# Reordering gate products, GpSimd weight steps and the last branch-B unit in a hybrid encoder block

## The chip, the cores and the metric

The kernel runs on one core of one Trainium2 chip. The metric is device time in microseconds (us) of one execution. The engines are called PE (TensorE, matrix products), PEld (PE's weight loads), DVE (VectorE), ACT (ScalarE), POOL (GpSimd) and SP (SyncE, which mostly issues DMA transfers).

## The reference, cut to what matters

One encoder block on 1024 tokens plus 16 meta tokens, model width 1024. One projection feeds two attention branches and two gates; the gated sum goes through an output projection and then a SwiGLU feed-forward.

```python
proj = h @ w_in                       # qa, ka, va, qb, kb, vb, ga, gb
y_a = differential_attention(qa, ka, va, ...)   # 4 heads, two score maps each, all 1040 keys
y_b = windowed_gqa(qb, kb, vb, sink)            # 8 heads in 2 groups, keys within 128
merged = jax.nn.sigmoid(ga) * (y_a @ w_ba) + jax.nn.sigmoid(gb) * (y_b @ w_bb)
h = h + merged @ w_o                  # then the feed-forward
```

The differential attention takes softmax(map 1) - lam * softmax(map 2), times v, and a norm over the head. All data are float32; the kernel splits each operand of a product into a high and a low part and adds three matmuls (high x high, high x low, low x high).

## The kernel before, in words

**Branch B** (`attend_b`, lines 363 to 465) works in units (g, t): group g, 128-token block t. A unit computes scores, softmax and transposes, and its `finish()` accumulates the values into one PSUM bank `bpy`. For the key tile with the meta tokens (k = 8) ACT makes the high part `bmh` (L443) and DVE the low part in four pieces, `btm` (L446); PE's first values matmul (L447) waits for these. At its end ACT copies one half of `bpy` (L459), DVE adds the other (L460), and SP stores the result to `yb_d` in DRAM (L461). Units overlap: the copy and add of unit (1,6) are queued in the middle of unit (1,7), the last.

**Branch A** (the loop of lines 1136 to 1178) works in 32 tiles: head h of 4, token block t of 8. A string of `SLOTS` gives the order of PE's steps in a tile: `s` is a scores step (matmuls L1028; DVE then takes L1031, L1035), `t` a group of transposes of the previous tile (`apt` L1057, taken by ACT L1060 and DVE L1061 into `at`), `n` a step of values or norm, and `g` a quarter of a gate product. Tiles 0 to 15 use the first two strings in turn, tiles 16 to 31 the third, `SLOTS[2]`.

**The gates** (lines 757 to 965) and half of the columns of qa are computed as 2 x 2 block products in the manner of Strassen and Winograd: each of nine column pairs k (0 to 7, and `Q_PAIR` = 8) takes seven products p. `order_g` lists them in two passes. The first, `first_g`, has products 1, 6 and 2 of each k; the second has products 5, 3, 7 and 4. A product is 4 steps of 3 matmuls (L921) against the transposed input `hT` (high and low parts in SBUF).
- Its weights are made on POOL by `weights_g`: block sums of the raw weights (L806 to L819), a rounded high part (L828) and a low part (L829). The four operand buffers are freed by PE; the raw weights are loaded by SP (`load_g`, L786).
- Its result is built up in one of two PSUM banks, `pp0` and `pp1`. Products 1 and 2 of a k share a bank, and so do 5 and 3, and 7 and 4. Between the two of a pair another engine reads the bank: ACT copies after 1 (L927) and 5 (`q`, L949), DVE adds after 6 (L945) and 7 (`g`, L952). Product 5 begins in a bank that ACT has loaded with a kept sum (L904).
- Between the passes SP replaces quarters of `hT` by block sums that were stored in DRAM as `t_d[0..3]` (`turn_into`, L853), each as soon as the last product that needs the old quarter is done (`LAST_T`).
- All other stores and loads of this stretch go through SP's one queue in program order.

The order in which the scheduler hands an instruction to an engine's queue is held by two means: `queue_behind` (one instruction after another on the same engine) and `tc.issue_after` blocks.

Of the kernel before, what the change touches and what calls it, by code (L numbers as in the profile page):

```python
# [74 lines left out]
def encoder_block(ctx: ExitStack, tc: tile.TileContext, x, meta, norm_mix, w_in, lq1, lk1, lq2, lk2,  # L75
# [289 lines left out]
    scaled = []  # L365
    last_unit, quarters = [], []

# [29 lines left out]
    def attend_b(g, t, qb):  # L397
# [33 lines left out]
        def finish():  # L431
            py = bank(psum1, "by", f"bpy_{nm}", 1)
            for k in [8, *range(b0, b1)]:
# [4 lines left out]
                if k == 8:  # L438
                    steps[-1].append(nc.tensor.transpose(pt[:, 0, :], md, ident))
                    steps.append([])  # L440
                    tm = tms[t % 2]
                    hi = bpool.tile([P, P], F32R, tag="bmh", name=f"bmh_{nm}", bufs=1)
                    nc.scalar.activation(hi, pt[:, 0, :], AF.Copy, scale=of_hi)  # L443
                    for r in range(4):
                        at = slice(32 * r, 32 * r + 32)
                        nc.vector.scalar_tensor_tensor(tm[at, r], pt[at, 0, :], of_x[at], f32(hi[at]), ALU.mult, ALU.subtract)  # L446
                    steps[-1].append(nc.tensor.matmul(py, vb[g][:, 8, :], tm.rearrange("p r t -> p (r t)"), start=True, stop=False))  # L447
                    continue
# [6 lines left out]
                for hl in range(2):  # L455
                    steps[-1].append(nc.tensor.matmul(py, vb[g][:, k, :], tr[:, hl].rearrange("p r t -> p (r t)"),  # L456
                                                      start=False, stop=(k == b1 - 1 and hl == 1)))
            y1 = bpool.tile([64, 512], F32, tag="by1", name=f"by1_{nm}", bufs=2)
            nc.scalar.copy(y1, py[64:128])  # L459
            nc.vector.tensor_tensor(y1, py[0:64], y1, ALU.add)  # L460
            nc.sync.dma_start(yb_d[g][:, t * P:(t + 1) * P].rearrange("(r d) t -> d r t", r=4),  # L461
                              y1.rearrange("d (r t) -> d r t", r=4))
        return finish
# [295 lines left out]
    for k in (2, 3, 4, 5, 6, Q_PAIR):  # L759
        first_g += [(k, 1), (k, 6), (k, 2)] + ([(0, 6)] if k == 6 else [])  # L760
    first_g += [(7, 1), (7, 2), (7, 6), (1, 6)]
    second_g = [Q_PAIR, *range(8)]
    behind_g = dict(zip(second_g, second_g[1:]))
    order_g = first_g + [(k, p) for k in second_g for p in (5, 3, 7, 4)]
    n_first = len(first_g)

    uses_g = []
    for n, (k, p) in enumerate(order_g):
        if n >= n_first:
            uses_g.append([("s", k, 1), ("s", k, 0)] if p == 5 else [])  # L770
        else:
            uses_g.append({1: [("f", k, 0)], 2: [], 6: [("f", k, 1)] if k >= N_SPLIT else [("m", k, 0), ("m", k, 1)]}[p])
    loads_g = [u for us in uses_g for u in us]
    raw_g, ops_g, n_loaded, n_freed, n_made = {}, {}, [0], [0], [0]

    def load_g():
        while n_loaded[0] < min(len(loads_g), n_freed[0] + 4):
            kind, k, i = key = loads_g[n_loaded[0]]
            p, tag = ((wpool, "w"), (gwork, "w2"))[n_loaded[0] // 2 % 2]
            n_loaded[0] += 1  # L780
            col = G_COLS[k] + i * P
            w = raw_g[key] = p.tile([P, DC, P], F32, tag=tag, name=f"wg_{kind}{k}_{i}", bufs=2)
            with ExitStack() as after:
                if n_loaded[0] > 4:
                    after.enter_context(tc.issue_after(keys_a[0].ins))
                raws_g.append(nc.sync.dma_start(w, w_in[:, col:col + P].rearrange("(c p) n -> p c n", p=P)))  # L786

    sums_g, keys_a, raws_g, values_in, turned_t, made_g = {}, [], [], [], {}, []

    def weights_g(n):  # L790
# [11 lines left out]
        elif p == 2:  # L802
            src = a12
            n_freed[0] += 1 if k < N_SPLIT else 2 if k != 7 else 0
        elif p == 6:
            tt(a21, a21, a22, ALU.add)  # L806
            tt(a21, a21, a11, ALU.subtract)
            src = a21
            if k < N_SPLIT or k == 7:
                n_freed[0] += 2  # L810
# [13 lines left out]
        op = ops_g[n] = wpool.tile([P, 2, 4, P], F32R, tag=("wh", "wl")[n % 2], name=f"wopg_{nm}", bufs=W_BUFS)  # L824
        with ExitStack() as after:
            if made_g:
                after.enter_context(tc.issue_after(made_g[-1].ins))
            nc.gpsimd.tensor_copy(op[:, 0], src)  # L828
            made_g.append(tt(op[:, 1], src, f32(op[:, 0]), ALU.subtract))  # L829
# [26 lines left out]
    def gate_steps():  # L856
# [1072 lines left out]
```

## Time and profile before

| | |
|---|---|
| median of 3 runs (range) | 1433.23 us (1431.43 to 1435.07) |
| profiled execution, its span | 1433.91 us, 1432.0 us |
| PE busy | 1405.1 us, 98% of the span |
| DVE, ACT, POOL busy | 927.9, 671.5, 656.4 us |
| longest stretch with PE never idle | 626.5 to 1425 |

An execution runs through the projections and branch B (to about 284 us), branch A with the gate products between its steps (284 to 626), the gated output projection and the feed-forward (from 626). A row of the profile's timeline gives start, duration, engine, line, operation and tiles; in brackets stands how long the engine sat idle before it and what ended the wait.

### The profile page before, as it was taken

Reading aid. Unit: us, or ns where it says so; the run is one execution under the profiler, and the core shown is the slowest. Engines: PE = TensorE matmul, PEld = TensorE weight load, DVE = VectorE, ACT = ScalarE, POOL = GpSimd, SP = SyncE. Lnnn points to the kernel's source line nnn. Section 1 sums busy time; section 2 is a strip of 40 time slices with the busy share of each in tenths; the row PEclk is TensorE's granted clock in tenths of the full one; section 3 lists DMA queues with packets and bytes.
Section 4 is the critical chain, followed back from the end, with each engine's and each line's share of the span. In section 5 each row is a group of like instructions: output and inputs, shape, how many; then the busy total and the mean of one; then the engine's idle time right before and its main releaser. Section 6 shows DMA issues by size and latency. Waiting matters only on the chain.

```text
span 1432.0 us, 20674 instructions
## 1 busy us (share of the span) xinstructions
PE 1405.1 (98%) x7171; PEld 1203.1 (84%) x7171; DVE 927.9 (65%) x1587; ACT 671.5 (47%) x1285; POOL 656.4 (46%) x666
## 2 busy tenths in 40 slices
PE   9999999999999999999999999999999999999998
PEld 8989999888888788878888888888888888888886
DVE  6547676667667767655978966655544553787566
ACT  6346555444444445455346654333333333444454
POOL 4157884476677667331603044444545442000442
PEclk9999999999999999999999999999999999999999
DMA  8446558463796353197341624423332232954333
GB/s 236 101 120 187 176 184 285 118 200 123 246 326 210 114 193 110 46 318 236 115 154 74 206 89 142 152 96 111 103 104 101 98 103 103 347 197 140 125 126 147
DMA packets 192953, 227.73 MB, mean 159 GB/s; under 512 B 16889, under 2 KB 126401, under 8 KB 192721
## 3 DMA queue, kind: packets, MB, share of 16 engines
q1 hardware_dynamic: 190928, 223.59, 48.4%
q10 hardware_dynamic: 1920, 2.83, 0.7%
q8 instruction: 56, 0.92, 0.3%
q14 instruction: 49, 0.39, 0.1%
HBM read 152.48 MB, written 68.39 MB: 154 GB/s over the span
## 4 chain that ended last, share of the span: by engine, by line
PE 88%; DMA 4%; DVE 3%; POOL 2%; issue 1%; ACT 1%; SPq 0%; DVEq 0%; ACTq 0%; POOLq 0%
PE pg L1692 29%; PE pd L1796 14%; PE pg L921 9%; PE ppa L743 6%; PE po L1595 4%; PE aps L1028 3%; PE pp_qb L232 3%; PE apy L1070 3%; PE pp_va L232 2%; PE apt L1057 2%; PE pp_ka L232 2%; PE pp_qa L232 2%; PE po L1603 2%; PE bpy L456 1%; PE bps L412 1%
## 5 line engine op out<-in xcount | busy, mean ns | idle before, releaser
L1692 PE MATMUL pg<-t,wop 128*128 128x512 f32 x1056 | 242.4, 389 | 0.0
L1692 PEld LDWEIGHTS pg<-t,wop 128*128 128x128 f32 x1056 | 198.2, 188 | 41.2
L121 POOL TENSOR_TENSOR wop<-wf,wop 128x512 fp32r<-128x512 f32 x114 | 150.3, 1319 | 165.1 <-ACT wop L120 155.1
L1796 PE MATMUL pd<-ob,oa 128*128 128x512 f32 x924 | 209.8, 389 | 0.0
L1796 PEld LDWEIGHTS pd<-ob,oa 128*128 128x128 f32 x924 | 173.4, 188 | 36.3 <-DVE ob L121 0.3
L921 PE MATMUL pg<-hT_hi,wopg 128*128 128x512 f32 x504 | 191.1, 404 | 13.0 <-DVE g L952 7.1
L1692 PE MATMUL pg<-b,wop 128*128 128x512 f32 x792 | 183.3, 389 | 0.0
L1692 PEld LDWEIGHTS pg<-b,wop 128*128 128x128 f32 x792 | 148.4, 188 | 30.7
L921 PEld LDWEIGHTS pg<-hT_hi,wopg 128*128 128x128 f32 x504 | 95.1, 189 | 33.2 <-DVE g L952 7.9
L1039 ACT ACTIVATE as<-as,amn 128x1040 f32<-128x1040 f32 x64 | 74.6, 1165 | 88.1 <-DVE amn L1035 86.6
L120 ACT ACTIVATE wop<-wf 128x512 fp32r<-128x512 f32 x128 | 80.7, 632 | 72.9 <-PE pg L1692 51.3
L121 POOL TENSOR_TENSOR oa<-ra,oa 128x512 fp32r<-128x512 f32 x27 | 34.9, 1294 | 168.9 <-ACT oa L120 167.4
L921 PE MATMUL pg<-hT_lo,wopg 128*128 128x512 f32 x252 | 99.6, 395 | 0.2 <-DMA hT_lo<-t_d 0.2
L120 ACT ACTIVATE oa<-ra 128x512 fp32r<-128x512 f32 x77 | 48.7, 632 | 107.5 <-PE pd L1796 50.7
L1028 PE MATMUL aps<-ak,aq 128*128 128x352 f32 (+1 forms) x384 | 87.0, 335 | 0.6 <-DVE amn L1031 0.4
L1469 DVE TENSOR_TENSOR s<-wf,wf 128x512 f32<-128x512 f32 x22 | 15.9, 725 | 109.5 <-DMA wf<-in_w_ff_up_dram 69.8
L1031 DVE CUSTOM_DVE_ANT_0 as<-aps,dist,far_a 128x704 f32<-128x704 f32 x64 | 60.3, 942 | 22.2 <-PE aps L1028 22.0
L1028 PEld LDWEIGHTS aps<-ak,aq 128*128 128x128 f32 x384 | 64.6, 190 | 9.4 <-DVE amn L1031 1.7
L414 DVE CUSTOM_DVE_ANT_0 bs<-bps,tbx,nsink 128x432 f32<-128x432 f32 (+1 forms) x64 | 38.3, 627 | 43.4 <-PE bps L412 31.3
L1060 ACT ACTIVATE at<-apt 128x512 fp32r<-128x512 f32 (+1 forms) x96 | 45.8, 486 | 42.0 <-PE apt L1057 41.6
L424 POOL TENSOR_SCALAR bs<-bs,bdn 128x432 f32<-128x432 f32 (+1 forms) x64 | 37.1, 601 | 52.4 <-DVE bdn L422 31.9
L1070 PEld LDWEIGHTS apy<-at,av 128*128 128x128 f32 x400 | 54.9, 192 | 4.2
(327 smaller groups left out, 3115.5 us busy)
## 6 DMA issues: line engine op xcount, KB each, us to landing
ra<-aop SPq DMA_DIRECT2D x77, 256.0 KB, 2.6
wf<-in_w_ff_gate_dram SPq DMA_DIRECT2D x25, 512.0 KB, 3.6
wf<-in_w_ff_up_dram SPq DMA_DIRECT2D x25, 512.0 KB, 3.6
aop<-as SPq DMA_DIRECT2D x44, 256.0 KB, 2.1
wg_s<-in_w_in_dram SPq DMA_DIRECT2D x18, 512.0 KB, 4.6
aop<-c SPq DMA_DIRECT2D x33, 256.0 KB, 2.0
ak<-ka_d SPq DMA_DIRECT2D x16, 520.0 KB, 6.7
t_d<-tst SPq DMA_DIRECT2D x16, 512.0 KB, 4.8
```

The lines of the kernel that those rows point to most:

```text
L120: high = nc.scalar.activation(hi, src, AF.Copy)
L121: lo_eng.tensor_tensor(lo, src, f32(hi), ALU.subtract)
L232: product = nc.tensor.matmul(ps[:, :n], a[:, c, :], b[:, c, at:at + n], start=(u == 0), stop=(u == 3 * DC - 1))
L743: nc.tensor.matmul(ps, w[:, a, j, :], src(j, b, tk), start=(j == 0 and n == 0), stop=(j == 3 and n == 2))
L921: product = nc.tensor.matmul(ps, op[:, x, c, :], h[:, 4 * d + c, HALF[t]], start=(p in (1, 6, 7) and c == 0 and i == 0), stop=(p in (2, 6, ...
L1028: nc.tensor.matmul(ps[:, :n], qs[m][:, t * P:(t + 1) * P], ks[m][:, vv, k0:k0 + n], start=(vv == 0), stop=(vv == 1))
L1031: nc.vector.tensor_tensor_reduce(s[m][:, 0:2 * n].rearrange("p (a k) -> p a k", a=2), two[:, :, :n], dist[:, u0:u0 + 2 * n].rearrange("p ( ...
L1039: nc.scalar.activation(s[m][:, 0:L], s[m][:, 0:L], AF.Exp, bias=mn[:, m, 1:2], scale=-1.0, accum_out=dn[:, 1:2] if m else first_sum)
L1070: nc.tensor.matmul(py[:, cols], v[:kp, a, k, :], at_[:kp, k, b, :], start=(k == 0 and j == 0), stop=(k == 8))
L1595: nc.tensor.matmul(sets_o[p][u], oa[:, a, u * P:(u + 1) * P], ob[:, b, :], start=(p in (1, 5) and j == 0 and k == 0), stop=(p in (2, 3) an ...
L1692: nc.tensor.matmul(ps, op[:, x, c, :], b[:, y, c, :], start=(p in (1, 5) and c == 0 and n == 0), stop=(p in (4, 2, 3) and c == 3 and n == ...
L1796: nc.tensor.matmul(ps[u], oa[:, a, u * P:(u + 1) * P], ob[:, b, :], start=(p in (1, 2, 5) and j == 0 and k == 0), stop=(p in (2, 3, 4) and ...
```

## The change

Six edits, all in the stretch from about 276 to 626 us:

1. In `weights_g` the order given to POOL covered the rounding and the low part only, so the block sums of later products could stand earlier in the queue. Now all steps of a product stand behind the last step of the product before.
2. The end of the first pass, (0,6) ... (7,1) (7,2) (7,6) (1,6), becomes (0,6) ... (1,6) (7,1) (7,6) (7,2).
3. The second pass runs each k as 5, 7, 3, 4 instead of 5, 3, 7, 4.
4. The quarter of `hT` that comes from `t_d[1]` is replaced after (7,6) and that from `t_d[3]` after (7,2); the loads of kept sums move to other products (`k_next`).
5. The last unit of branch B takes a scores bank (`bs`) for `bpy`; the copy and add of unit (1,6) are queued behind `bmh` and the last `btm` of (1,7); the store of (1,7) is issued by ACT instead of SP.
6. In `SLOTS[2]` the first transposes of a tile stand behind both scores steps of the first map taken.

```diff
-SLOTS = "ssgsggntssgsggntgnt", "ssggsggntssgsggntgnt", "ssgsgntssgsgntgnt"
+SLOTS = "ssgsggntssgsggntgnt", "ssggsggntssgsggntgnt", "ssgsgnssgtsgntgnt"
...
-            py = bank(psum1, "by", f"bpy_{nm}", 1)
+            py = bank(psum1, *("by", f"bpy_{nm}", 1) if (g, t) != (BG - 1, NT - 1) else ("bs", f"bpy_{nm}", 2))
...
+                    if (g, t) == (BG - 1, NT - 1):
+                        for late, first in zip(sums_b[-1], (high, low)):
+                            queue_behind([late], first)
...
-            nc.scalar.copy(y1, py[64:128])
-            nc.vector.tensor_tensor(y1, py[0:64], y1, ALU.add)
-            nc.sync.dma_start(yb_d[g][:, t * P:(t + 1) * P].rearrange("(r d) t -> d r t", r=4),
+            sums_b.append((nc.scalar.copy(y1, py[64:128]), nc.vector.tensor_tensor(y1, py[0:64], y1, ALU.add)))
+            queue = nc.scalar if (g, t) == (BG - 1, NT - 1) else nc.sync
+            queue.dma_start(yb_d[g][:, t * P:(t + 1) * P].rearrange("(r d) t -> d r t", r=4),
...
-        first_g += [(k, 1), (k, 6), (k, 2)] + ([(0, 6)] if k == 6 else [])
-    first_g += [(7, 1), (7, 2), (7, 6), (1, 6)]
+        first_g += [(k, 1), (k, 6), (k, 2)] + ([(k != 6, 6)] if k > 5 else [])
+    first_g += [(7, 1), (7, 6), (7, 2)]
...
-    order_g = first_g + [(k, p) for k in second_g for p in (5, 3, 7, 4)]
+    order_g = first_g + [(k, p) for k in second_g for p in (5, 7, 3, 4)]
...
-        with ExitStack() as after:
-            if made_g:
-                after.enter_context(tc.issue_after(made_g[-1].ins))
-            nc.gpsimd.tensor_copy(op[:, 0], src)
-            made_g.append(tt(op[:, 1], src, f32(op[:, 0]), ALU.subtract))
+        nc.gpsimd.tensor_copy(op[:, 0], src)
+        made_g.append(tt(op[:, 1], src, f32(op[:, 0]), ALU.subtract))
...
         while n_made[0] < min(n, len(order_g)):
-            weights_g(n_made[0])
+            with ExitStack() as after:
+                if made_g:
+                    after.enter_context(tc.issue_after(made_g[-1].ins))
+                weights_g(n_made[0])
...
-    LAST_T = {(0, 1): (2,), (7, 1): (0,), (7, 2): (3,), (1, 6): (1,)}
+    LAST_T = {(0, 1): (2,), (7, 1): (0,), (7, 6): (1,), (7, 2): (3,)}
...
+                    elif i == 1:
+                        after.enter_context(tc.issue_after(load_of["s", Q_PAIR, 0].ins))
...
-            k_next = {(6, 6): 0, (7, 1): 1, (7, 2): Q_PAIR}.get((k, p), behind_g.get(k) if p == 3 else None)
+            k_next = {(6, 6): 0, (Q_PAIR, 6): 1, (7, 1): Q_PAIR}.get((k, p), behind_g.get(k) if p == 7 else None)
```

The added lines shift the line numbers by 3 to 7 behind line 443: the gate matmul L921 is L928 in the kernel after, and L1028, L1057 and L1070 are L1035, L1064 and L1077.

ACT's queue at the end of branch B, before; `by1_1_6` and `by1_1_7` are the output copies of units (1,6) and (1,7), `p1_0` the copy after gate product (0,1):

```order
L453 ACTIVATE btr_1_6_7_2460<-bpt_1_6_7_2455 128x512
L459 COPY by1_1_6_2465<-bpy_1_6_2425 64x512
L443 ACTIVATE bmh_1_7_2472<-bpt_1_7_8_2470,columns_161 128x128
L453 ACTIVATE btr_1_7_6_2484<-bpt_1_7_6_2479 128x512
L453 ACTIVATE btr_1_7_7_2494<-bpt_1_7_7_2489 128x512
L459 COPY by1_1_7_2499<-bpy_1_7_2469 64x512
L927 COPY p1_0_3495<-pg_0_1_3482 128x512
L927 COPY p1_1_3513<-pg_1_1_3500 128x512
```

The same place after:

```order
L456 ACTIVATE btr_1_6_7_2460<-bpt_1_6_7_2455 128x512
L443 ACTIVATE bmh_1_7_2472<-bpt_1_7_8_2470,columns_161 128x128
L462 COPY by1_1_6_2465<-bpy_1_6_2425 64x512
L456 ACTIVATE btr_1_7_6_2484<-bpt_1_7_6_2479 128x512
L456 ACTIVATE btr_1_7_7_2494<-bpt_1_7_7_2489 128x512
L462 COPY by1_1_7_2499<-bpy_1_7_2469 64x512
L464 DMA yb_d1_110<-by1_1_7_2499 64x4x128
L934 COPY p1_0_3495<-pg_0_1_3482 128x512
L934 COPY p1_1_3513<-pg_1_1_3500 128x512
```

`bmh` of the last unit now stands ahead of the copy of (1,6), and ACT issues the store of (1,7) ahead of the copy of product (0,1).

POOL's queue in the first pass around the weights of (8,6), before; `wg_f8` and `wg_f7` are raw weights of k = 8 and 7, `wopg_8_6` the operand of product (8,6):

```order
L806 TENSOR_TENSOR wg_f8_1_4240<-wg_f8_1_4240 128x512
L807 TENSOR_TENSOR wg_f8_1_4240<-wg_f8_1_4240,wg_f8_0_4238 128x512
L828 CAST wopg_8_6_4346<-wg_f8_1_4240 128x512
L975 COPY far_m2_3431<-dist_852 128x320
L806 TENSOR_TENSOR wg_f7_1_4312<-wg_f7_1_4312 128x512
L829 TENSOR_TENSOR wopg_8_6_4346<-wg_f8_1_4240,wopg_8_6_4346 128x512
L828 CAST wopg_8_2_4397<-wg_f8_0_4238 128x512
L1046 COPY as0_0_3437<-as0_0_3437 128x32
L807 TENSOR_TENSOR wg_f7_1_4312<-wg_f7_1_4312,wg_f7_0_4310 128x512
```

The same place after (products (1,6) and its raw weights `wg_m` carry `True` for 1 in their names):

```order
L811 TENSOR_TENSOR wg_f8_1_4240<-wg_f8_1_4240 128x512
L812 TENSOR_TENSOR wg_f8_1_4240<-wg_f8_1_4240,wg_f8_0_4238 128x512
L830 CAST wopg_8_6_4346<-wg_f8_1_4240 128x512
L982 COPY far_m2_3431<-dist_852 128x320
L831 TENSOR_TENSOR wopg_8_6_4346<-wg_f8_1_4240,wopg_8_6_4346 128x512
L830 CAST wopg_8_2_4397<-wg_f8_0_4238 128x512
L1053 COPY as0_0_3437<-as0_0_3437 128x32
L831 TENSOR_TENSOR wopg_8_2_4397<-wg_f8_0_4238,wopg_8_2_4397 128x512
L811 TENSOR_TENSOR wg_mTrue_1_4312<-wg_mTrue_1_4312 128x512
L812 TENSOR_TENSOR wg_mTrue_1_4312<-wg_mTrue_1_4312,wg_mTrue_0_4310 128x512
```

The block sum on `wg_f7_1` no longer stands between the two parts of (8,6)'s operand; each product's sums follow the low part of the product before.

PE's queue in the second pass at block k = 8, before: the end of product (8,5) and the start of (8,3), which writes the bank `pg_8_5` again (`wopg_8_3` is its operand):

```order
L921 MATMUL pg_8_5_4732<-hT_lo_140,wopg_8_5_4691 128x512
L921 MATMUL pg_8_5_4732<-hT_hi_139,wopg_8_5_4691 128x512
L1070 MATMUL apy_1_1_4755<-at1_0_4332,av1_4297 128x256 x7
L1057 MATMUL apt_1_3_1_4858<-ident_111,as0_1_3438 128x128 x4
L921 MATMUL pg_8_5_4732<-hT_hi_139,wopg_8_3_4729 128x512
L921 MATMUL pg_8_5_4732<-hT_lo_140,wopg_8_3_4729 128x512
L921 MATMUL pg_8_5_4732<-hT_hi_139,wopg_8_3_4729 128x512
L1057 MATMUL apt_1_3_2_4873<-ident_111,as0_1_3438 128x128
L1028 MATMUL aps2_1_5_1_4884<-ak1_1_4288,aq1_1_4287 128x352 x4
```

The same place after:

```order
L928 MATMUL pg_8_5_4737<-hT_lo_140,wopg_8_5_4689 128x512
L928 MATMUL pg_8_5_4737<-hT_hi_139,wopg_8_5_4689 128x512
L1077 MATMUL apy_1_1_4759<-at1_0_4332,av1_4297 128x256 x7
L1064 MATMUL apt_1_3_1_4858<-ident_111,as0_1_3438 128x128 x4
L928 MATMUL pg_8_7_4870<-hT_hi_139,wopg_8_7_4734 128x512
L928 MATMUL pg_8_7_4870<-hT_lo_140,wopg_8_7_4734 128x512
L928 MATMUL pg_8_7_4870<-hT_hi_139,wopg_8_7_4734 128x512
L1064 MATMUL apt_1_3_2_4874<-ident_111,as0_1_3438 128x128
L1035 MATMUL aps2_1_5_1_4885<-ak1_1_4288,aq1_1_4287 128x352 x4
```

Behind the last quarter of (8,5) now come the first quarters of (8,7) in the other bank; (8,3) follows one product later, in the places that (8,7) had.

More of the change, by code (lines that the diff above doesn't have):

```diff
@@ L365, in encoder_block @@
     scaled = []
-    last_unit, quarters = [], []
+    last_unit, quarters, sums_b = [], [], []
     def queue_behind(late, first):
@@ L442, in finish @@
                     hi = bpool.tile([P, P], F32R, tag="bmh", name=f"bmh_{nm}", bufs=1)
-                    nc.scalar.activation(hi, pt[:, 0, :], AF.Copy, scale=of_hi)
+                    high = nc.scalar.activation(hi, pt[:, 0, :], AF.Copy, scale=of_hi)
                     for r in range(4):
                         at = slice(32 * r, 32 * r + 32)
-                        nc.vector.scalar_tensor_tensor(tm[at, r], pt[at, 0, :], of_x[at], f32(hi[at]), ALU.mult, ALU.subtract)
+                        low = nc.vector.scalar_tensor_tensor(tm[at, r], pt[at, 0, :], of_x[at], f32(hi[at]), ALU.mult, ALU.subtract)
+                    if (g, t) == (BG - 1, NT - 1):
+                        for late, first in zip(sums_b[-1], (high, low)):
+                            queue_behind([late], first)
                     steps[-1].append(nc.tensor.matmul(py, vb[g][:, 8, :], tm.rearrange("p r t -> p (r t)"), start=True, stop=False))
@@ L803, in weights_g @@
             src = a12
-            n_freed[0] += 1 if k < N_SPLIT else 2 if k != 7 else 0
+            n_freed[0] += 1 if k < N_SPLIT else 2
         elif p == 6:
@@ L808, in weights_g @@
             src = a21
-            if k < N_SPLIT or k == 7:
+            if k < N_SPLIT:
                 n_freed[0] += 2
```

4 lines of the change are left out of this document (3 added, 1 removed).

## The prediction

> **What bounds the kernel now.** I read the page's busy times first, then busy time by stage, then the waits of TensorE (PE), then the timeline at each wait. Every time below is in us from the start of the profiled execution, whose own time was 1433.91 with a span of 1432.0; the 1.9 outside the span I leave alone. The median of the runs, 1433.23, lies 0.68 lower, so what I take off the profiled run I take off the median too.
>
> ```profile
> span 1432.0 us, 20674 instructions
> PE 1405.1 (98%) x7171; PEld 1203.1 (84%) x7171; DVE 927.9 (65%) x1587; ACT 671.5 (47%) x1285; POOL 656.4 (46%) x666
> ```
>
> ```profile
> 275.00:300.00 25.00, 20.89 (x86) 15.74 (x86) 10.55 (x24) 9.41 (x17) 13.45 (x21) 0.86 0.71 224
> ...
> 390.00:425.00 35.00, 32.76 (x192) 28.41 (x191) 22.97 (x52) 16.44 (x30) 26.31 (x28) 1.00 1.00 341
> 400.00:450.00 50.00, 47.48 (x281) 41.53 (x280) 37.78 (x79) 24.72 (x46) 38.68 (x41) 1.00 0.89 284
> 440.00:600.00 160.00, 151.01 (x905) 133.52 (x904) 114.46 (x261) 76.72 (x142) 100.63 (x115) 0.99 0.43 138
> 626.50:1425.00 798.50, 798.50 (x3555) 661.38 (x3554) 514.74 (x672) 351.56 (x624) 272.55 (x215) 1.00 0.43 143
> ```
>
> A row of the second view is a stretch, its length, the busy times of PE, PEld (weight loads), DVE (VectorE), ACT (ScalarE) and POOL (GpSimd), the granted PE clock, DMA share and GB/s. PE is never idle from 626.5 to 1425, and the change adds no arithmetic to any engine. So it can only win or lose the gaps of PE before 626.5, and a gap closed there reaches the end unchanged. All of PE's idle time is 1432.0 - 1405.1 = 26.9, which caps what closed gaps alone can give.
>
> ```profile
> PE pg L921 <- DVE g L952: 7.1, 5, 2.2
> PE pg L921 <- POOL wopg L829: 2.4, 3, 1.1
> PE bpy L447 <- DVE btm L446: 2.3, 1, 2.3
> PE pg L921 <- ACT q L949: 1.5, 4, 0.6
> ...
> PE apt L1057 <- DVE at L1061: 1.1, 2, 0.8
> ...
> PE pg L921 <- DVE p L945: 1.1, 1, 1.1
> PE pg L921 <- ACT p L927: 0.8, 1, 0.8
> PE aps L1028 <- DVE amn L1031: 0.4, 1, 0.4
> ```
>
> In TensorE's waits (total, times, longest) the gate products, L921, lead: they wait for the reader of the PSUM bank that they are to write again (DVE, ACT) or for their weights (POOL). The change is aimed at eight of these rows, 16.7 together. I cost them part by part.
>
> **1. Last unit of branch B.**
>
> ```profile
> 276.39 0.58 ACT L459 COPY by<-bpy 64x512 f32<-64x512 f32 x1 [3.70 <-PE bpy L456]
> 277.00 0.37 ACT L443 ACTIVATE bmh<-bpt,columns 128x128 fp32r<-128x128 f32 x1
> 277.01 0.68 DVE L460 TENSOR_TENSOR by<-bpy,by 64x512 f32<-64x512 f32 x1 [3.49 <-ACT by L459]
> 277.62 1.43 DVE L446 SCALAR_TENSOR_TENSOR btm<-bpt,columns,bmh 32x128 fp32r<-32x128 f32 x4
> 277.72 7.66 SPq L461 DMA_DIRECT2D yb_d<-by  x2
> 279.19 0.77 PE L447 MATMUL bpy<-btm,vb 128*128 128x512 f32 x1 [2.29 <-DVE btm L446]
> ...
> 284.08 1.07 ACT L927 COPY p<-pg 128x512 f32<-128x512 f32 x2
> 284.72 0.79 PE L921 MATMUL pg<-hT_hi,wopg 128*128 128x512 f32 x1
> ```
>
> The copy (0.58) and add (0.68) of the previous unit go behind bmh and the four btm. bmh can then start at about 276.5 and btm at 276.9 instead of 277.62, so PE resumes about 0.7 sooner: the wait of 2.29 becomes about 1.55. The bank taken from the scores pool adds no wait, since its next user comes long after. But the store of this unit moves from SP's queue to ACT's. There it waits for the DVE add of its own unit, and behind it stands the copy p (L927) that releases the bank PE needs at 284.72. Nobody else waits for the store itself. Price: the add, 0.68, plus an issue on ACT, for which the nearest row is this:
>
> ```profile
> 17.39 0.37 ACTq L482 DMA_DIRECT2D x<-in_x_dram  x1
> ```
>
> Say 1.05 against the 0.7 won. The clock decides the rest.
>
> ```profile
> 278.90:285.70 6.80, 6.14 (x15) 4.23 (x16) 3.07 (x6) 2.25 (x4) 2.54 (x2) 0.50 0.13 35
> 500.75:504.16 3.41, 3.35 (x12) 3.06 (x13) 0.65 (x4) 1.25 (x2) 3.41 (x5) 0.50 0.67 204
> ...
> 500.08 0.67 DVE L952 TENSOR_TENSOR g<-pg,q 128x512 f32<-128x512 f32 x1
> 500.81 0.80 PE L921 MATMUL pg<-hT_hi,wopg 128*128 128x512 f32 x1 [2.23 <-DVE g L952]
> 502.26 2.08 PE L1070 MATMUL apy<-at,av 128*128 128x256 f32 x9
> ...
> 530.07 0.50 PE L921 MATMUL pg<-hT_hi,wopg 128*128 128x512 f32 x1 [1.70 <-DVE g L952]
> ...
> 581.97 1.23 PE L1070 MATMUL apy<-at,av 128*128 128x256 f32 x9
> ```
>
> The granted clock was 0.50 just behind the two waits over 2.2 (2.29 and 2.23) and stayed full behind the wait of 1.70: nine apy took 2.08 in the slow stretch and 1.23 at full clock. So a stretch of 3.41 at half clock costs about 3.35 / 2 = 1.7. At 1.55 this stage should keep its clock. Redone with full-clock durations, the first step of product (0,2) comes at about 283.95 instead of 284.72, and the rest of the slow stretch, to 285.70, takes half as long, another 0.5. I take a gain of 1.3; bounds: a loss of 0.5 (clock not kept, ACT's wait paid) to a gain of 3.
>
> [...]
>
> **2. GpSimd's steps in product order, SP freed earlier.**
>
> ```profile
> 373.78 1.29 POOL L806 TENSOR_TENSOR wg_f<-wg_f 128x512 f32<-128x512 f32 x1
> 375.03 2.27 POOL L829 TENSOR_TENSOR wopg<-wg_f,wopg 128x512 fp32r<-128x512 f32 x1
> 377.35 0.50 PE L921 MATMUL pg<-hT_hi,wopg 128*128 128x512 f32 x1 [1.12 <-POOL wopg L829]
> ...
> 291.18 1.30 POOL L806 TENSOR_TENSOR wg_f<-wg_f 128x512 f32<-128x512 f32 x1 [0.91 <-DMA wg_f<-in_w_in_dram]
> 293.75 0.50 PE L921 MATMUL pg<-hT_hi,wopg 128*128 128x512 f32 x1 [1.10 <-POOL wopg L829]
> ```
>
> At 377.35 PE waited 1.12 for the low part of (8,6)'s weights, which had stood behind a 1.29 add of a later product; the change puts that add behind it, so 1.12 goes. At 293.75 POOL had waited for a load that SP could not issue while it sat in the yb_d store (7.66 from 277.72). That store leaves SP, so the load comes several us sooner and POOL's cover is back. The three waits on POOL are 2.4. I take 2.0; ends 2.4 and -1, because a POOL that no longer works ahead on raw weights has an add of 1.29 more to do whenever a weight buffer frees late.
>
> **3. End of the first pass.** Before, (7,2) follows (7,1) in one bank and waits 0.77 for ACT's copy; (1,6) waits 1.13 for DVE's add on the bank of (7,6). In the new order another product stands between each pair.
>
> ```profile
> 404.44 0.47 PE L921 MATMUL pg<-hT_hi,wopg 128*128 128x512 f32 x1 [1.13 <-DVE p L945]
> ...
> 417.31 0.47 PE L921 MATMUL pg<-hT_hi,wopg 128*128 128x512 f32 x1 [0.34 <-ACT q L949]
> ```
>
> From the first to the second row are two products, so a product lasts about 6.4 with the attention steps between; copy and add end within about 1.9. Gain 1.9 (0.8 + 1.1), lower end 1.
>
> **4. Second pass, (5,3,7,4) to (5,7,3,4).** (3) writes the bank of (5) again, and (4) that of (7). Before, these stand next to each other, and so PE waits for the copy q (L949) and the add g (L952). Afterwards a whole product lies between. The last block, k=7, ran in the new order already; its waits are these:
>
> ```profile
> 619.69 0.50 PE L921 MATMUL pg<-hT_hi,wopg 128*128 128x512 f32 x1 [0.18 <-ACT q L949]
> ...
> 623.55 0.47 PE L921 MATMUL pg<-hT_hi,wopg 128*128 128x512 f32 x1 [0.84 <-DVE g L952]
> ```
>
> They remain. There the cover is a product without attention steps, 623.55 - 619.69 = 3.86 with its wait; elsewhere it is about 6. What goes is 7.1 - 0.84 + 1.5 - 0.18 = 7.6, and the half-clock stretch at 500.75, 1.7: 9.3. What comes: the bank of the next block's (5) now frees only while (4) runs, and ACT must in that time copy g of (3) and load the kept sum (two copies of that size took 1.07, L927's row above) between attention's own steps. And DVE, busy 114.46 of 160 here, has its g adds behind attention's: at 500.81 the add itself takes 0.67 of a 2.23 wait. I put this at 3 (eight blocks, nearly 0.4 each); ends 0 and 7.6, the whole gain of waits. Net 6.3.
>
> **5. SLOTS[2]** puts a tile's first transposes behind both score steps of map 0, in 16 tiles. The waits for at and amn, 1.1 + 0.4, are likely to go, but the second scores reach their single bank earlier. Take +1; ends +1.5 and -3.5 (an estimate: 0.2 in each tile).
>
> **6. Reloads of hT.** t_d0, t_d1 and t_d3 (each twice 128 x 4 x 512 words of 4 bytes, 2.1 MB) now lie closer together, with two raw weights of 0.5 MB between; with smaller transfers 8.3 MB in all. With the gains of parts 1 to 3 off, (8,5), which begins near 404.44 + 6.4 = 410.9 in the trace, comes near 405, and (8,4), three products of about 6 later, near 422. The reload can begin two products ahead of (8,5), at 394.5 with 5 each. The stage moved 341 GB/s at a full DMA share (390 to 425): 8.3 MB take 24.3 and end near 419, in time. At 284, the next row, they end near 424: a wait of 2. I take -1, from 0 to -7 (32 at 256 GB/s, an estimate below both rows: a wait of 5, and a half-clock stretch).
>
> [...]
>
> Sum: 1.3 + 2.0 + 1.9 + 6.3 + 1.0 - 1.0 = 11.5 off 1433.9. The half-clock trigger also needs no wait over 2.2 to appear anywhere; one new one in eight blocks costs 1.7, so I keep 10.5: 1423.4, or 1422.7 against the median; rounded, 1423.
>
> **The rivals.** *Slots turn against PE* (ends slower): scores go first, so DVE does amn and the far part before the at adds, and PE's values steps wait for at. For it speaks that DVE is the busiest engine beside PE in 440 to 600 and that at and amn already appear among PE's waits; against it, that they come to only 1.5 in 32 tiles. Elsewhere 10.5 - 1.0 = 9.5 are won, so it decides from 0.6 per tile in 16 tiles, and shows as slower from (9.5 + 4.3) / 16 = 0.9. With two adds of 0.67 uncovered, 1.35 per tile, it costs 21.6: 1433 + 21.6 - 9.5 = 1445.
>
> *The bank of the next block becomes the wait*: ACT's two copies arrive late in eight blocks and part 4 comes to nothing: 1423 + 6.3 = 1429.3.
>
> *Reload late*: 256 GB/s or less, term 6 at -7 to -10: about 1430.5.
>
> *The slow stretches stay*, because something other than the waits ahead of them sets the clock (two such waits and one of 1.70 without it are all the evidence): 1423 + 1.7 + 0.8 = 1425.5. [...]
>
> *Everything closes*: 16.7 of waits less 1.55 (btm) and 1.0 (block 7), and 2.2 of clock: 1433.2 - 16.4 = 1417.
>
> **How the numbers follow.** Forecast 0.49 (own range 1419 to 1428.5), slots 0.11, bank of the next block 0.13, reload 0.09, slow stretches 0.08, everything closes 0.10. A measurement of this kernel can tell about 0.3%, 4.3 us, from no change, so faster is below 1428.9 and slower above 1437.5. Faster: 0.45 of the forecast, 0.08, 0.10 and 0.05 of the bank's: 0.68. Slower: 0.11 and 0.02 of a worse reload: 0.13. Within: 0.19. The range is 1415 to 1435: it leaves out the slots rival and some 0.06 at its lower end.
>
> **What would show it.** Right: TensorE's waits for DVE g fall below 2 and for POOL wopg below 0.5; no stretch at clock 0.5 at 500; the btm wait is near 1.6; the first product behind branch B starts near 284. Wrong: rows of PE waiting for ACT's kept copy (L904 of before) or for DMA on hT, waits for at summing over 5, or a new 0.5 stretch.

## The result, and the profile after

The changed kernel takes 1422.22 us (median; 1421.53 to 1423.53) against 1433.27 for the kernel before in the same comparison: a ratio of 0.9922, 95% interval 0.9909 to 0.9935. That is 11.05 faster. The forecast was 1423.0 with a range of 1415 to 1435. The total was right, but two groups of its terms were not: one was missed by 5.0 in the wrong direction, the other by 4.5 in the other. That the two misses nearly cancel is luck.

The page's head after, span and busy times by engine:

```profile
span 1420.5 us, 20697 instructions
PE 1400.6 (99%) x7171; PEld 1201.6 (85%) x7171; DVE 920.5 (65%) x1587; ACT 674.6 (47%) x1285; POOL 657.9 (46%) x666
```

The span is 11.5 shorter. To see where, I cut both traces at the same four gate products: the starts of (0,1), (8,2), (8,5) and (7,4). Each row is a stretch with its length and the busy times of PE, PEld, DVE, ACT and POOL; the products in corresponding rows are the same. Before:

```profile
268.07:382.54 114.47, 109.23 (x588) 93.07 (x587) 71.06 (x157) 48.97 (x91) 76.49 (x93) 0.97 0.57 179
382.54:410.33 27.79, 25.89 (x153) 22.36 (x152) 19.51 (x44) 13.11 (x24) 16.69 (x20) 1.00 0.85 284
410.33:623.55 213.22, 202.88 (x1207) 178.62 (x1206) 150.09 (x329) 104.91 (x194) 137.68 (x152) 0.99 0.50 161
```

After:

```profile
267.21:383.40 116.19, 109.45 (x588) 93.22 (x587) 70.23 (x157) 49.28 (x91) 74.55 (x91) 0.97 0.56 180
383.40:409.36 25.96, 25.65 (x153) 22.52 (x152) 20.09 (x47) 12.60 (x23) 18.08 (x21) 1.00 0.80 265
409.36:611.77 202.41, 199.20 (x1208) 176.62 (x1206) 148.17 (x326) 107.35 (x194) 138.50 (x152) 1.00 0.52 174
```

| stretch | parts of the prediction in it | forecast | measured |
|---|---|---|---|
| end of branch B and first pass, to (8,2) | 1 and 2 | 3.3 faster | 1.7 slower (114.47 to 116.19) |
| end of the first pass | 3 | 1.9 faster | 1.8 faster (27.79 to 25.96) |
| second pass | 4, 5 and 6 | 6.3 faster | 10.8 faster (213.22 to 202.41) |

Ahead of (0,1) the trace after is 0.86 shorter. The order there is unchanged, and the wait that makes the difference (1.2, a transpose for DVE's `btr`) is absent or present in runs of either kind, so I count it as chance. With that the table gives 0.9 - 1.7 + 1.8 + 10.8 = 11.8 at (7,4), and 0.3 is lost again after it, which leaves the 11.5 of the span.

PE's waits after (total, times, longest), line numbers 3 to 7 higher than before:

```profile
PE pg L928 <- ACT p L934: 2.1, 1, 2.1
PE pg L928 <- DVE g L959: 1.7, 1, 1.7
PE bpy L450 <- DVE btm L446: 1.5, 1, 1.5
PE pg L928 <- POOL wopg L831: 1.5, 4, 0.6
PE pg L928 <- POOL wopg L830: 1.3, 1, 1.3
...
PE aps L1035 <- DVE amn L1038: 1.2, 5, 0.2
...
PE pg L928 <- ACT g L948: 0.4, 1, 0.4
...
PE apt L1064 <- DVE at L1068: 0.2, 1, 0.2
```

The waits for the add g fell from 7.1 to 1.7 (the one of block 7 that was expected to stay, grown from 0.84), those for the copy q from 1.5 to nothing that shows, and the two at the end of the first pass are gone. Two waits are new: 2.1 for ACT's copy p of product (0,1) (the 0.8 of that row before was the wait at (7,2)), and 1.3 for POOL's rounded part L830. Both, and 0.6 of L831's 1.5, end between 283 and 300.1. This is the timeline there, with PE's rows as the engine's own timeline gives them:

```profile
277.58 0.50 PE L450 MATMUL bpy<-btm,vb 128*128 128x512 f32 x1 [1.53 <-DVE btm L446]
...
278.95 1.25 SPq L790 DMA_DIRECT2D wg_f<-in_w_in_dram  x2
280.25 1.07 SPq L860 DMA_DIRECT2D hT_hi<-t_d  x1
281.37 0.89 SPq L860 DMA_DIRECT2D hT_lo<-t_d  x1
282.02 0.68 ACTq L464 DMA_DIRECT2D yb_d<-by  x1
282.74 1.07 ACT L934 COPY p<-pg 128x512 f32<-128x512 f32 x2 [1.46 <-DVE by L462]
283.38 0.79 PE L928 MATMUL pg<-hT_hi,wopg 128*128 128x512 f32 x1 [2.08 <-ACT p L934]
290.30 0.11 POOL L985 MEMSET far_m<- 128x16 f32 x1 [16.13 <-issue]
298.69 0.50 PE L928 MATMUL pg<-hT_hi,wopg 128*128 128x512 f32 x1 [1.31 <-POOL wopg L830]
300.04 0.50 PE L928 MATMUL pg<-hT_hi,wopg 128*128 128x512 f32 x1 [0.62 <-POOL wopg L831]
```

The same place before:

```profile
284.80 0.57 SPq L461 DMA_DIRECT2D yb_d<-by  x1
285.47 1.27 SPq L786 DMA_DIRECT2D wg_f<-in_w_in_dram  x2
...
287.39 0.11 POOL L978 MEMSET far_m<- 128x16 f32 x1 [4.35 <-issue]
```

Before, SP issued the store of the last branch-B tile first and its loads behind it, and POOL's first `far_m` started 2.6 after the store's issue. After, the store is issued 2.8 earlier (282.02), by ACT, but SP's loads of 3 MB are already on their way, and `far_m` starts 8.3 after the store's issue, 2.9 later than before. Behind `far_m`, POOL's queue holds the weights of the next products, and DVE's L1042 waits 7.97 for it too. That POOL waits for this store is a reading of the trace so far; the experiments test it.

### The profile page after: what moved, and what is told of

The parts are those of the page before. It is cut to its first block, busy times and chain, and to the rows that moved or that the text cites. A ratio compares the mean times of both kernels' runs of the same rounds, so it can differ in the third digit from the quotient of the medians.

```text
span 1420.5 us, 20697 instructions
## 1 busy us (share of the span) xinstructions
PE 1400.6 (99%) x7171; PEld 1201.6 (85%) x7171; DVE 920.5 (65%) x1587; ACT 674.6 (47%) x1285; POOL 657.9 (46%) x666
## 4 chain that ended last, share of the span: by engine, by line
PE 73%; DVE 2%; POOL 1%; DMA 1%; issue 1%; ACT 1%; SPq 0%; DVEq 0%; POOLq 0%; ACTq 0%
PE pg L1699 29%; PE pd L1803 15%; PE pg L928 8%; PE ppa L746 6%; PE po L1602 4%; PE aps L1035 3%; PE apy L1077 3%; PE apt L1064 2%; PE po L1610 2%; DVE as L1052 1%; ACT as L1046 1%; POOL wopg L831 1%; DMA g_d<-g 1%; PE ptn_f L1567 0%; DVE as L1038 0%
## 5 line engine op out<-in xcount | busy, mean ns | idle before, releaser
L928 PE MATMUL pg<-hT_hi,wopg 128*128 128x512 f32 x488 | 185.2, 405 | 7.0 <-ACT p L934 2.1
L928 PEld LDWEIGHTS pg<-hT_hi,wopg 128*128 128x128 f32 x488 | 92.4, 190 | 24.6 <-POOL wopg L831 3.5
L928 PE MATMUL pg<-hT_lo,wopg 128*128 128x512 f32 x244 | 96.5, 396 | 0.0
L1035 PE MATMUL aps<-ak,aq 128*128 128x352 f32 (+1 forms) x384 | 87.5, 336 | 1.2 <-DVE amn L1038 1.2
L1035 PEld LDWEIGHTS aps<-ak,aq 128*128 128x128 f32 x384 | 64.2, 191 | 9.8 <-DVE amn L1038 3.2
L1726 ACT COPY p<-pg 128x512 f32<-128x512 f32 x44 | 25.8, 587 | 66.6 <-PE pg L1699 66.6
```

Of the source, the lines that this page charges most:

```text
L928: product = nc.tensor.matmul(ps, op[:, x, c, :], h[:, 4 * d + c, HALF[t]], start=(p in (1, 6, 7) and c == 0 and i == 0), stop=(p in (2, 6, ...
L1035: nc.tensor.matmul(ps[:, :n], qs[m][:, t * P:(t + 1) * P], ks[m][:, vv, k0:k0 + n], start=(vv == 0), stop=(vv == 1))
```

## The experiments

All were compared with the kernel before, measured on the same chip in the same comparison (medians 1432.4 to 1432.8 there). Ratios stand with their 95% interval. The changed kernel, in its own comparison, has 0.9922 (0.9909 to 0.9935), so it is set against a run here by the ratios. The profiled execution of e3 took 4.8 more than the median of its runs and that of e2 3.2 less; each kernel has one trace.

| run | median | ratio to before |
|---|---|---|
| e1: before + second pass order | 1425.9 | 0.9947 (0.9934 to 0.9960) |
| e2: before + slots | 1431.8 | 0.9990 (0.9979 to 1.0001) |
| e3: before + unit B edits | 1435.9 | 1.0025 (1.0013 to 1.0036) |
| e4: before + POOL order | 1431.9 | 0.9998 (0.9989 to 1.0006) |
| e5: before + end of first pass | 1432.6 | 0.9999 (0.9989 to 1.0009) |
| e9: before + POOL order + end of first pass | 1431.4 | 0.9994 (0.9985 to 1.0003) |
| e10: after, old slots | 1424.0 | 0.9942 (0.9930 to 0.9955) |
| e6: after, last store issued by SP | 1418.1 | 0.9898 (0.9885 to 0.9911) |
| e7: after, far_m placed elsewhere | 1416.8 | 0.9894 (0.9881 to 0.9906) |
| e8: e6 and e7 together | 1416.8 | 0.9888 (0.9874 to 0.9903) |
| e11: e8 + six filling matmuls | 1416.4 | 0.9891 (0.9875 to 0.9906) |
| e12: e7 + six filling matmuls | 1417.8 | 0.9887 (0.9868 to 0.9906) |

### Does the last store of branch B hold POOL? (e3, e7, e6, e8)

**e3**: the edits to unit (1,7) alone.

```diff
-            nc.sync.dma_start(yb_d[g]...
+            queue = nc.scalar if (g, t) == (BG - 1, NT - 1) else nc.sync
+            queue.dma_start(yb_d[g]...
...
+                            queue_behind([late], first)
```

> The kernel before with only the edits to the last unit of branch B (scores bank, copy and add queued later, store issued by ACT). Theory A: the store issued by ACT comes after SP's 3 MB of loads and lands about 8 us after its issue; the first far_m of POOL, which lies where the stored tile lay, waits for it until about 290, and PE's copy of product (0,1) waits behind the issue on ACT; the clock drops again. The btm wait falls to 1.5, but the kernel becomes 2 to 3 slower: 1435.5. Theory B (the late POOL steps of the changed kernel near 298 come from the strict order of GpSimd's steps): far_m at 285, the kernel 1.3 faster: 1432.

It was 3.6 slower by the ratio (1.9 to 5.2): theory A. The btm wait is 1.54, PE waits 2.08 for the copy p, and `far_m` comes as late as in the changed kernel: 22.6 behind the start of (0,1) at 270.4, where it is 23.1 there and 19.3 in the kernel before.

```profile
292.98 0.11 POOL L981 MEMSET far_m<- 128x16 f32 x1 [7.85 <-DMA hT_hi<-t_d]
```

Theory B had no place for that, since this kernel has the old POOL order. One detail of A was wrong: in this trace the clock did not drop behind the 2.08 wait; it dropped later, at 298.41 for 3.41. The profile puts the end of POOL's wait down to a load of hT. e6 below speaks against that: there `far_m` starts 0.58 after the issue of that load (284.59), and such loads take 9.3 from issue to landing (median in the trace after).

**e7**: the changed kernel with one allocation moved. Branch A's pool takes over the memory of branch B's; on the reading above, `far_m` lay on the tile that the last store reads. With the at buffers behind it, it lies elsewhere.

```diff
-    apool.tile([P, 9, 2, 256], F32R, tag="at", name="at_room", bufs=AT_BUFS)
     far_m = [(gstage if i > 1 else apool).tile([P, 336], F32, name=f"far_m{i}") for i in range(3)]
...
         nc.gpsimd.memset(s0s[i][:, L + 2 * NM:], 0.0)
+    apool.tile([P, 9, 2, 256], F32R, tag="at", name="at_room", bufs=AT_BUFS)
```

> The changed kernel with one allocation moved: the at buffers are placed behind far_m and as0 in branch A's memory, so that far_m no longer lies where the stored tile of branch B lay. The store stays on ACT. Theory A: far_m starts within 1 us of the end of POOL's earlier work (about 281 to 285) though the store lands as late as before; POOL waits of 0.4 + 1.3 + 0.6 near 293 to 300 go, ACT's wait of 2.08 and the half clock stay: 1420.0. Theory B: nothing changes, 1422.

```profile
273.62 0.12 POOL L984 MEMSET far_m<- 128x16 f32 x1
...
278.40 0.11 POOL L984 MEMSET far_m<- 128x16 f32 x1 [3.83 <-PE bpt L453]
...
281.85 0.68 ACTq L464 DMA_DIRECT2D yb_d<-by  x1
...
283.20 0.79 PE L928 MATMUL pg<-hT_hi,wopg 128*128 128x512 f32 x1 [1.55 <-ACT p L934]
```

The first of the three fills of `far_m` starts at 273.62, straight behind POOL's earlier work, and the last at 278.40, all ahead of the store's issue at 281.85; no wait for POOL near 293 to 300 is left, and ACT's wait is there, at 1.55. So it was the place of `far_m` in memory that held POOL, and e6 shows that the store is what held the place. The kernel is 4.0 faster than the changed one by the ratios (5.5 by the medians), more than the 2.2 expected: in its trace 4.9 is won ahead of (8,2).

**e6**: the other way round, the placement as in the change and the store back on SP.

```diff
-            queue = nc.scalar if (g, t) == (BG - 1, NT - 1) else nc.sync
+            queue = nc.sync
```

> The changed kernel with the last store of branch B issued by SP again, ahead of its loads. Theory A (the ACT store lands late and blocks ACT): far_m starts near 284.5 instead of 290.3, PE's wait of 2.08 for ACT's copy is about 0.6, no half-clock stretch behind it, POOL waits near 298 gone: 4 to 5 faster than the changed kernel, 1417.5 to 1418.5. Theory B (strict POOL order): only ACT's wait and the clock, and POOL still late at 298: 1419 to 1420. Theory C: the loads behind the store come later and POOL waits for them as before (1.1): 1419.

```profile
278.85 4.33 SPq L464 DMA_DIRECT2D yb_d<-by  x2
...
285.17 0.11 POOL L985 MEMSET far_m<- 128x16 f32 x1 [10.42 <-issue]
```

Ahead of the loads the store lets `far_m` start at 285.17; ACT's wait is 0.64, no half-clock stretch follows. But the loads wait behind the store in SP's queue, and PE waits 1.09 for POOL and 0.69 for hT a little later. So A and C both hold, and 1418.1 lies where they meet; by the ratio the gain over the changed kernel is 3.4, with intervals that touch. **e8** has both edits:

> Both: far_m placed elsewhere and the store issued by SP. Theory A: ACT's wait, the half clock and POOL's waits all go, 1416 to 1417. Theory C of the run before it: the loads behind the store come 3 us later than with the ACT store and POOL waits for them: 1418.

1416.8, the same as e7: with `far_m` placed elsewhere, which queue issues the store no longer matters to the time. A named the time, but one of its steps did not come: the half clock stayed, 6.83 from 278.69, now right behind the wait for btm.

### What each part is worth alone (e1, e2, e4, e5, e9, e10)

**e1**:

```diff
-    order_g = first_g + [(k, p) for k in second_g for p in (5, 3, 7, 4)]
+    order_g = first_g + [(k, p) for k in second_g for p in (5, 7, 3, 4)]
...
-            k_next = {...}.get((k, p), behind_g.get(k) if p == 3 else None)
+            k_next = {...}.get((k, p), behind_g.get(k) if p == 7 else None)
```

> The kernel before with only the second pass in the order 5, 7, 3, 4 (and the loads of kept sums moved to product 7). Theory A (no wait takes the place of the ones removed): PE's waits for the add g (6.2 of 7.1) and the copy q (1.4 of 1.5) go and the half-clock stretch near 500 goes, together 9.3; time 1424.0. Theory B (the prediction's term: about 3 come back as waits for ACT's two bank copies and for DVE): 6.3 less, 1427.0, with rows of PE waiting for the kept copy.

7.6 faster by the ratio (5.7 to 9.5), between the two theories, for a reason that neither had. In its trace the second pass lasts from 409.85 to 615.26, 7.8 less than before. Its waits of PE:

```profile
PE pg L921 <- DMA hT_hi<-t_d: 1.8, 2, 1.0
...
PE pg L921 <- DVE g L952: 0.9, 1, 0.9
```

The waits for g and q are gone as in A and nothing waits for the kept copy; but the quarter of hT from `t_d[1]` is now needed one product earlier while it is still loaded last, and PE waits 1.8 for it. The change's other order of reloads removes that: in its trace no PE row waits for hT there.

**e2** is one string:

```diff
-SLOTS = "ssgsggntssgsggntgnt", "ssggsggntssgsggntgnt", "ssgsgntssgsgntgnt"
+SLOTS = "ssgsggntssgsggntgnt", "ssggsggntssgsggntgnt", "ssgsgnssgtsgntgnt"
```

> The kernel before with only the third slot string changed. Theory A: only the three waits of PE for at and amn, 1.5 together, can go: 1431.8. Theory B (the rival of the prediction): PE waits for at or amn at most tiles from the 17th on: 1440 or more. Theory C: the trace of the changed kernel won 11.7 in the second pass where its waits and the clock were worth 9.3, so the slots give the other 2.4: 1430.9.

1.4 faster, with an interval from 3.0 faster to 0.1 slower: the rival that ended slower (0.6 or more per tile) is out, A and C can't be told apart. **e10** takes the same edit out of the changed kernel:

> The changed kernel with the old third slot string. Theory A: the slots are worth only their waits, 1.5 for at and amn against the 1.0 for amn that remain: 0.5 to 1 slower than the changed kernel, 1423. Theory B: they give DVE time in the second pass, 2.5 or more: 1424.7 or more, with waits of PE for DVE's g adds coming back.

1424.0, slower than the changed kernel by 1.8 by the medians and 2.9 by the ratios, though the intervals overlap, so the time alone does not choose between A and B. Waits for at and amn are back, and only 0.6 for g:

```profile
PE aps L1035 <- DVE amn L1038: 1.8, 6, 0.4
PE apt L1064 <- DVE at L1068: 1.6, 2, 0.8
```

That is 2.0 more than with the new string (1.2 + 0.2), and the wait for g, which B wanted back, is 1.1 less. So it is A's mechanism. To (7,4) the trace is 2.1 longer, counted from (0,1), but 1.0 of that lies ahead of tile 16 (451.2 in both traces), where the strings are the same and e10 has two half-clock stretches (10.24 and 3.41) for the one of 6.83. Behind it 1.1 is left as the price of the old string, a little above what A said.

**e4** and **e5** each take one part of the first pass, **e9** both.

```diff
# e4, e9
         while n_made[0] < min(n, len(order_g)):
-            weights_g(n_made[0])
+            with ExitStack() as after:
+                if made_g:
+                    after.enter_context(tc.issue_after(made_g[-1].ins))
+                weights_g(n_made[0])
# e5, e9
-    first_g += [(7, 1), (7, 2), (7, 6), (1, 6)]      # (1, 6) now behind (Q_PAIR, 2)
+    first_g += [(7, 1), (7, 6), (7, 2)]
-    LAST_T = {(0, 1): (2,), (7, 1): (0,), (7, 2): (3,), (1, 6): (1,)}
+    LAST_T = {(0, 1): (2,), (7, 1): (0,), (7, 6): (1,), (7, 2): (3,)}
```

> The kernel before with only the block sums of a product held behind the low part of the product before. Theory A: the wait of 1.12 at product (8,6) goes, the three waits near 294 to 298 stay as they depend on loads that SP issues late: 1432.1. Theory B: strict order makes POOL late at the start of branch A: waits of PE for POOL's weights of 2 or more there, 1435 or more.

> The kernel before with only the end of the first pass re-ordered (with the reloads of hT and the loads of kept sums that go with it). Prediction's term: the waits of 0.77 and 1.13 go: 1.9 faster, 1431.3. Rival (reload late): PE rows waiting for DMA on hT at the first products of the second pass, 2 to 7 slower than that.

> The kernel before with two edits together: GpSimd's steps in product order and the re-ordered end of the first pass. Each alone gave nothing (ratios 0.9998 and 0.9999). Theory A (they need each other: with the re-ordered end alone POOL came late, 2.7 of new waits near 401 and a half-clock stretch): the waits of 0.77, 1.13 and 1.12 all go with at most 0.3 of new ones near 400: 1429.5 to 1430.5. Theory B (gains of the first pass are given back in the second whatever the POOL order): 1432.5.

None of the three differs from the kernel before by more than its interval. e4 did more than its theory A said: the waits for POOL fell from 2.4 to 0.4, those near 294 to 298 included, while the wait for hT grew from 0.2 to 0.8; its (8,5) comes 1.2 earlier than before, counted from (0,1), and 0.9 of that is lost again in the second pass. e5 lost what it won at once: the waits of 0.77 and 1.13 went, and these came (e5's waits of PE):

```profile
PE pg L925 <- POOL wopg L831: 3.5, 4, 1.4
...
PE pg L925 <- POOL wopg L830: 2.1, 2, 1.8
```

Its (8,5) comes 2.5 later than before.

In e9 the two parts together did what A said up to the start of the second pass: all three waits are gone and 0.3 is left for POOL. Its (8,5) starts 4.0 earlier than in the kernel before, counted from (0,1). By the end 2.5 of that was given back, as B said: in the old second pass the waits for DVE's g and ACT's q grew by 0.5 and 0.3, and a second half-clock stretch came at 447.56 (the mean granted clock was 0.994 over e9's 1430.4, 0.995 over 1432.0 before).

```profile
PE pg L925 <- DVE g L956: 7.6, 6, 1.9
...
PE pg L925 <- ACT q L953: 1.8, 4, 0.7
```

One profile each shows this; the ratios alone don't tell these three runs from each other.

### What drops the clock (e11, e12)

The stretches at half clock are 3.41, 6.83 or 10.24 long in the traces here (6.83 and 3.41 before, 6.83 after, 10.24 and 3.41 in e10; the last one, which the kernel's end cuts off, aside), whole multiples of 3.41. So I read windows of that length ahead of stretches, placed by the edges of the half-clock stretches in the same trace: length, then PE busy; the granted clock is the third number from the end. From the kernel before, e2, e10 and e8, in this order:

```profile
497.34:500.75 3.41, 1.24 (x7) 0.83 (x5) 3.41 (x7) 0.00 (x0) 3.41 (x4) 1.00 0.00 0
500.75:504.16 3.41, 3.35 (x12) 3.06 (x13) 0.65 (x4) 1.25 (x2) 3.41 (x5) 0.50 0.67 204
```

```profile
493.60:497.01 3.41, 1.62 (x9) 1.21 (x8) 3.41 (x6) 0.28 (x1) 3.41 (x3) 1.00 0.01 2
497.01:500.42 3.41, 2.94 (x18) 2.76 (x19) 1.29 (x5) 1.26 (x2) 3.41 (x5) 1.00 0.55 155
```

```profile
295.24:298.65 3.41, 1.65 (x7) 0.73 (x5) 2.78 (x5) 0.42 (x1) 2.17 (x4) 1.00 0.20 77
298.65:302.06 3.41, 3.25 (x11) 2.97 (x12) 0.55 (x2) 1.90 (x4) 2.49 (x4) 0.50 0.53 156
```

```profile
275.28:278.69 3.41, 1.70 (x8) 0.98 (x7) 2.68 (x7) 1.83 (x4) 0.55 (x4) 1.00 0.67 186
278.69:282.10 3.41, 3.29 (x8) 2.21 (x9) 1.91 (x3) 1.66 (x3) 0.16 (x1) 0.50 0.19 43
```

PE busy for 1.24, 1.65 and 1.70 of 3.41 was followed by half clock, and 1.62 in e2 was not; nor was 1.62 in e3, in the window with its 2.08 wait (284.76 to 288.17). The trace after goes further:

```profile
275.36:278.78 3.42, 1.85 (x12) 1.24 (x10) 2.61 (x6) 1.55 (x3) 0.00 (x0) 1.00 0.83 239
278.78:282.19 3.41, 2.14 (x7) 1.18 (x7) 1.63 (x4) 1.18 (x2) 0.00 (x0) 1.00 0.67 177
282.19:285.60 3.41, 2.22 (x6) 1.93 (x7) 0.67 (x2) 1.07 (x2) 0.00 (x0) 0.50 1.07 343
```

The window with the btm wait (1.85 busy) was followed by full clock, and the next one, with 2.14 busy, by half clock. e2's wait of 2.26 straddles two windows (493.60 to 500.42) and no half clock followed; e8's wait of 1.54 lies in one (275.28 to 278.69) and half clock followed. But PE's busy time does not sort the windows. Of the windows at full clock with the least PE work in the traces before and after, from 20 to 626, those with 1.24 (497.34), 1.43 (275.47) and 2.14 (278.78) were followed by half clock, and those with 1.72 (528.06), 1.75 (609.87), 1.85 (275.36) and 2.11 (295.84) were not. What decides there stays open.

**e11** fills the wait in e8:

```diff
+                    for _ in range(6 if (g, t) == (BG - 1, NT - 1) else 0):
+                        fills.append(nc.tensor.matmul(py, vb[g][:, 8, :], qb[t // 4][:, 0, :], start=True, stop=True))
                     steps[-1].append(nc.tensor.matmul(py, vb[g][:, 8, :], tm...
...
+                if k == b0 and fills:
+                    queue_behind(fills, steps[-1][-1])
```

> The kernel with far_m placed elsewhere and the last store issued by SP, plus six matmuls of 512 columns on PE in its wait for btm; they write the bank that the next product overwrites. Theory A (the granted clock falls when PE idles enough within one interval of a 3.4 us grid): the wait for btm shrinks to 0.4 or less, no half-clock stretch between 275 and 290, about 2.5 faster than without the fill: 1414.3. Theory B (the clock falls at the end of branch B for another reason): the stretch stays, 1416.8.

```profile
275.00:278.41 3.41, 3.27 (x17) 2.40 (x16) 1.85 (x5) 1.55 (x3) 0.43 (x2) 1.00 1.00 282
```

The row is a stretch of that length around the place of the old wait. In this trace A's signs came out: the wait for btm and the half clock are gone, and the clock stayed full to the kernel's last 5 us. But e6 kept its clock there without a fill (btm wait 1.53, PE busy for 1.47 of the 3.00 from 276 to 279, clock 1.00 there and on to 300), so one trace does not show that the fill did it. The gain did not come: 1416.4, no difference from e8. PE came sooner to weights (0.8) and hT (0.6) that SP loads behind the store. **e12** has the store on ACT again, so that these loads come sooner:

> As e11, but with the last store issued by ACT as in the changed kernel (far_m placed elsewhere, six matmuls in the wait for btm). In e11 the clock stayed full and only 0.5 was won in the trace, since PE then met POOL's weights (0.8) and hT (0.6) that are loaded behind the store on SP's queue. Theory A: with the store on ACT these loads come 3 us earlier and both waits go; the wait for ACT's copy (1.5 to 2.1) stays; if it does not drop the clock, 2 faster than e7 without the fill: 1414.5 to 1415. Theory B: the wait for ACT's copy idles PE enough to drop the clock by itself, and the time is e7's, 1416.8.

```profile
281.92:285.33 3.41, 1.33 (x7) 0.95 (x8) 1.55 (x3) 1.57 (x3) 0.24 (x1) 1.00 0.98 290
285.33:288.74 3.41, 3.41 (x10) 2.85 (x9) 0.58 (x2) 1.10 (x2) 2.82 (x3) 0.50 1.02 372
```

Theory B: half clock follows the window with the wait of 2.08 for ACT's copy (1.33 busy; in e3 a wait of the same length, with 1.62 busy, was followed by full clock), and the time, 1417.8, is e7's within its spread (ratio 0.9887 against 0.9894). e7, e8, e11 and e12 all beat both kernels, the changed one by 4 to 5 by the ratios, and can't be told from each other.

## Why the prediction was right in sum and wrong in two terms

**Part 1, wrong.** Its first half held: the btm wait is 1.53 (1.55 said). What stands ahead of ACT's copy p is, as said, the add and the store's issue, but at a higher price: from the start of the copy by to that of the copy p it is 2.05 (280.69 to 282.74) where it was 0.60 before, so 1.45 for the 1.05 said (the issue took 0.68 on ACT, the row used had 0.37), and PE waited 2.08. Two further steps failed. "Nobody else waits for the store itself" is the costlier: POOL's `far_m` waited, for the memory that the store reads (e6, e7). With `far_m` elsewhere the stretch to (8,2) takes 111.25 in e7 (266.74 to 377.99), which is 3.2 less than before, for the 3.3 that parts 1 and 2 promised; so this one step is worth 4.9 of their miss of 5.0. That 3.2 lies so near to 3.3 is partly chance, since e7 still has a half-clock stretch of 6.83. And "at 1.55 this stage should keep its clock" took the length of a wait for what sets the clock: in the trace after, the clock held through the window of the btm wait and fell one window later, at 282.19, for 6.83; in e7, e8 and e10 it fell behind the btm wait of 1.5 (in e8 at 278.69, the wait having ended at 276.85).

**Part 2, half right.** At (8,6) the 1.12 went as said. The other wait was to go because SP's loads start sooner; they did (278.95 instead of 285.47), but just that put them ahead of the store. Parts 1 and 2 together were forecast at +3.3 and measured at -1.7, a miss of 5.0.

**Part 3, right in size**: 1.8 for 1.9. e5 and e9 add that it needs the POOL order of edit 1, which the prediction did not say.

**Parts 4 to 6, too small**: 10.8 for 6.3. The step that failed is "what comes: 3", a term that should have been near nothing: no wait for the kept copy appears, and DVE's lag shows only in block 7 (1.7). The runs give the total from two sides. By the experiments, e1's order alone takes 7.8 off the second pass, its 1.8 of waits for hT do not come in the change, and the slots are worth 1.1 (e10): 10.7. By the rows of that stretch, PE's idle time fell from 213.22 - 202.88 = 10.3 to 202.41 - 199.20 = 3.2, which is 7.1, and its busy time for the same work by 3.7. Of this, 1.7 is the half-clock stretch; the other 2.0 is only partly explained. Behind the wait at 530.07 in the trace before, the second matmul starts 0.33 after the first and the third 0.24 after the second; at 0.1 a wait, with 11 waits listed in that stretch before and 7 after, that is at most 1.1, an estimate that was not tried. Part 6's wait did not come (0 for -1), and part 5 was worth about 1 (e10), as said.

The rivals: slots against PE fell (e2), the bank of the next block fell (e1), the reload was late only without the change's own re-ordering (e1, 1.8), by its place in the order and not by the rate (338 GB/s from 390 to 425 after, 341 before). "Everything closes" came true for the second pass alone. "The slow stretches stay" was half true: the one at 500 went with its wait (in e1 too), the one at the end of branch B came again. Of the signs, the waits for g (below 2), the btm wait, the clock at 500 and the start of (0,2) near 284 came out as said; the waits for POOL, 2.8 where less than 0.5 was said, showed the error.

## What to carry to other kernels

The store here held the memory that it reads for 8.3 past its issue, and the next tile in that memory belonged to another engine; before a store moves to another queue, find what takes over its tile and which transfers will be in flight ahead of it. SP, freed of the store, issued its loads earlier (278.95 instead of 285.47), and they came ahead of the store (282.02) on which POOL waited. When a wait in one of several coupled orders is removed, measure the parts together: the start of (8,5) came 1.2 earlier with the POOL order alone (e4), 2.5 later with the new end of the pass alone (e5), and 4.0 earlier with both (e9).

## What the runs showed of the hardware that was not expected

- A store of 128 KB issued by ACT behind about 3 MB of SP's loads held its tile for 8.3 us; issued by SP ahead of them, for 2.6 (before), and in e6 `far_m` started 2.0 behind the end of its issue (278.85 + 4.33 = 283.18). The landing of the ACT store itself is not in the record; 8.3 is read from the start of `far_m`.
- The half-clock stretches are whole multiples of 3.41 us here (3.41, 6.83, 10.24), and the window ahead was not idle: PE was busy for 1.24 of it in the trace before (497.34) and for 2.14 in the trace after (278.78). Neither the length of a wait (no half clock followed 2.26 in e2, it followed 1.54 in e8) nor PE's busy time (none followed 1.85 in the trace after) tells alone which window half clock follows.
- With six matmuls in PE's wait (e11) no half clock followed it, and nothing measurable was won: PE then waited 0.8 for weights and 0.6 for hT.
